# Low parts of y and of the output weights on VectorE instead of GpSimd, their casts behind the newest gate's tanh, and the seventh pair's y split where it is gated

## The chip, the core and the metric

The kernel runs on one core of one Trainium2 chip. The metric is the device time of one execution in microseconds (us), as the median of several runs. Engines are named as the profile names them: PE is TensorE (matmuls; PEld are its weight loads), DVE is VectorE, ACT is ScalarE, POOL is GpSimd, SP is SyncE, whose queue issues the transfers.

## The reference, cut to what matters

A sequence of 1024 positions with 1024 channels passes through two residual layers and a final RMS norm, all in float32.

```python
# layer 0, RG-LRU (width 1536 = 12 blocks of 128)
u = h @ w_in;  xb, gate = u[..., :1536], u[..., 1536:]
xc = causal_depthwise_conv(xb, conv_w, conv_b)          # 4 taps
r = sigmoid(block_diag_linear(xc, wa, ba));  i = sigmoid(block_diag_linear(xc, wx, bx))
log_a = -8 * r * softplus(-a_param);  a = exp(log_a)
hs = associative_scan(a, sqrt(-expm1(2 * log_a)) * i * xc)
x = x + (hs * silu(gate)) @ w_out
# layer 1, forgetting attention (16 heads of 64)
q, k, v, gate, f = split(h @ w_in)
cum = cumsum(log_sigmoid(f + b_f))
p = softmax(mask(q k' / 8 + cum_q - cum_k));  o = p v
x = x + (o * silu(gate)) @ w_out
return rms_norm(x, final_g)
```

## The kernel before, in words

**Split matmuls.** Every float32 operand of a large matmul is held as two parts: a high part (`to_hi`, a cast to `fp32r`, mostly on ACT) and a low part (`to_lo`, the source less the high part, one subtraction of two SBUF tensors). A product is then three matmuls, high by high (L111), low weight by high (L112) and high weight by low (L113). So each weight tile needs a transfer, a cast and a subtraction before PE can use it, and PE waits for the subtraction one matmul later than for the cast. Weight tiles rotate through four buffers each of `wh` and `wl`, and three of `wf`, where the transfers land.

**Order.** The kernel is written as Python loops, and a scheduler puts each engine's instructions into one fixed list by its own timeline. On the chip each engine works through its list strictly in order. `tc.issue_after(i)` is a bound for the scheduler: what stands under it is placed behind instruction `i`.

**Layer 0** runs a loop over the 12 blocks, `n` from 0 to 11. Iteration `n` computes `ups` (block n's half of `u`, 48 matmuls), the two gates of block n-1 (`gates`: four `gate` products of three matmuls, each read by a tanh on ACT, first `th` in two halves, then `ti` in two halves; the products rotate through two PSUM banks, so that the first `ti` product needs the first `th` tanh done), block n-2's output y = a * sg (`outputs`: high part `yh` on ACT, low part `yl`), the convolution of block n (`us` on DVE, `xc`, three taps, `xch`, `xcl`), and `gps`, the gate half of `u` for block n-1. From n = 3 on, each iteration also does two pieces of the output projection of an earlier pair of blocks (`project_out`, one piece per `take(fill, 4)`): a piece loads one tile of output weights (`out_weights`: two transfers, the cast `wh` on ACT, the low part `wl`) and does four `ops` products of six matmuls. The first piece stands between `ups` and `gps`, the second behind `gps`. The recurrence (`recur`: activations L315 to L320, products L318, L319, L321 and the scan L322 on DVE) and `silu` (L299 to L301) run beside it.

**Layer 1** goes head by head, with `hd` from 0 to 15. The scores are made twice, once as `S` for the row maxima (L664 on DVE, an exponential on ACT at L667) and once transposed as `ST`, whose exponential `p` (L734, L737) gets masked on POOL (L742), split into `ph` and `pl` on DVE and multiplied by v into `O`. `gated` multiplies the output `yo` of a pair of heads by its gate on POOL (L777). For pairs 0 to 6 the result goes to DRAM (`y1d`), and `load_y` brings it back later and splits it into `yhh` and `yhl` for the last projection; only pair 7's is split where it stands, with `split_y`. `late`, a generator that runs beside head 14, loads the output weights of pairs 6 and 7, casts them (`woh` on ACT) and makes their low parts (`wol` on POOL), and then calls `load_y` for pair 6.

Of the kernel before, what the change touches and what calls it, by code (L numbers as in the profile page):

```python
# [33 lines left out]
def f32(ap):  # L34
    return ap.bitcast(F32)
# [3 lines left out]
def trunk(ctx: ExitStack, tc: tile.TileContext, xt, w0, wg, wo0, pc, gn, w1, wv, wf, bf, wo1, out):  # L39
    nc = tc.nc  # L40
# [31 lines left out]
    def to_hi(hi, src, eng, scale=None):  # L72
        if eng is nc.scalar:
            if scale is None:
                nc.scalar.copy(hi, src)  # L75
            else:
                nc.scalar.activation(hi, src, AF.Copy, scale=scale)
        elif eng is nc.gpsimd:
            nc.gpsimd.tensor_scalar(hi, src, 1.0 if scale is None else scale, 0.0, ALU.mult, ALU.add)
        elif scale is None:  # L80
            eng.tensor_copy(hi, src)  # L81
        else:
            eng.tensor_scalar(hi, src, scale, None, ALU.mult)

    def to_lo(lo, src, hi, eng):
        return eng.tensor_tensor(lo, src, f32(hi), ALU.subtract)  # L86
# [30 lines left out]
    def drain(gen):  # L117
        for _ in gen:
            pass
# [5 lines left out]
    def gemm(*args):  # L125
        drain(gemm_steps(*args))
# [42 lines left out]
    with ExitStack() as l0:  # L169
# [8 lines left out]
        def long(tag, dtype=F32, bufs=1):  # L178
            return tmp.tile([P, SEQ], dtype, tag=tag, name=tag, bufs=bufs)
# [101 lines left out]
        def gates(n):  # L281

            s = state[n]
            s["t"] = long("th"), long("ti")
            for j, b_ in enumerate((hba, hbx)):
                w = tuple(z[:, j] for z in s["w"])
                for cs in halves:
                    pt = ps.tile([P, HALF], F32, tag="O", name="gate")
                    gemm(pt, [(w, tuple(z[:, cs] for z in s["x"]))])
                    s["last"] = nc.scalar.activation(  # L290
                        s["t"][j][:, cs], pt, AF.Tanh, bias=b_[:, n : n + 1], scale=0.5
                    )

# [31 lines left out]
        def outputs(n, parts=(slice(0, SEQ),), gate=itertools.repeat(None)):  # L325
            s = state.pop(n)
            y = tuple(ypool.tile([P, SEQ], F32R, tag=z, name=z) for z in ("yh", "yl"))
            for cs, _ in zip(parts, gate):
                a_ = s["a"][:, cs]
                nc.vector.tensor_tensor(a_, a_, s["sg"][:, cs], ALU.mult)  # L330
                yh, yl = (z[:, cs] for z in y)
                to_hi(yh, a_, nc.scalar)
                to_lo(yl, a_, yh, nc.vector if len(parts) > 1 else nc.gpsimd)
            ys.append(y)

        def out_weights(g, d0):

            wt = wpool.tile([P, 4, P], F32, tag="wf", name="wf", bufs=3)
            for j in range(2):
                nc.sync.dma_start(wt[:, 2 * j : 2 * j + 2], wo0[d0 + j, :, 2 * g : 2 * g + 2])  # L340
            hi = wpool.tile([P, 4, P], F32R, tag="wh", name="wh")
            lo = wpool.tile([P, 4, P], F32R, tag="wl", name="wl")
            to_hi(hi, wt, nc.scalar)
            to_lo(lo, wt, hi, nc.vector if held is None else nc.gpsimd)
            return [[(hi[:, 2 * j + i], lo[:, 2 * j + i]) for i in range(2)] for j in range(2)]

        def project_out(g):

            for d0 in range(0, KT, 2):
                for db, w in enumerate(out_weights(g, d0), d0):  # L350
                    for h, cs in enumerate(halves):
                        pt = ps.tile([P, HALF], F32, tag="g", name="ops")
                        gemm(pt, zip(w, [tuple(z[:, cs] for z in p) for p in ys[2 * g : 2 * g + 2]]))
                        x = xs[h][db]
                        nc.vector.tensor_tensor(x, x, pt, ALU.add)  # L355
                        yield
# [3 lines left out]

        ys, fill, held = [], iter(()), {}
        for n in range(NB):
            wu = first[0] if n == 0 else list(weights(w0[n]))
            if n == 1:
# [24 lines left out]
            if n % 2 and n > 1:  # L391
                fill = itertools.chain(fill, project_out((n - 3) // 2))
# [15 lines left out]
        for h in range(2):  # L408
            product(gps[:, h], h, wn)
        outputs(NB - 2)  # L410
        held = None
        drain(fill)
        recur(NB - 1, halves)
        outputs(NB - 1, halves, silu(state[NB - 1], gps, halves))
# [17 lines left out]
        wl = [w for d0 in range(0, KT, 2) for w in out_weights(NB // 2 - 1, d0)]  # L432
        for h, cs in enumerate(halves):
            y = [tuple(z[:, cs] for z in p) for p in ys[-2:]]
            hT[h] = [pair() for k in range(KT)]
            parts = split_x(h, 1)
# [29 lines left out]
    with ExitStack() as l1:  # L466
# [126 lines left out]
        parts = [at.tile([HEADS, SEQ], F32R, tag=t, name="cp") for t in ("ph", "pl")]  # L593
# [177 lines left out]
        def gated(hd, c, sub=slice(0, HALF)):  # L771

            if hd % 2 == 0:
                return
            pair = hd // 2
            yo = yos[pair, c][:, sub]
            nc.gpsimd.tensor_tensor(  # L777
                yo, yo, sgs[pair][:, c * HALF + sub.start : c * HALF + sub.stop], ALU.mult
            )
            if hd == 15:  # L780
                split_y(c, yo, nc.vector, sub)
            else:
                nc.sync.dma_start(y1d[c, pair], yo)

        def chain(*gens):
            for g in gens:
                yield from g

        last, seen, lag = [None], [None], []
# [20 lines left out]
        def load_y(c, pairs):  # L810
            for pair in pairs:
                y = at.tile([P, HALF], F32, tag="xp", name="y", bufs=3)
                nc.sync.dma_start(y, y1d[c, pair])
                split_y(c, y, nc.vector)
# [77 lines left out]
        def late():  # L892

            for half in range(2):
                wh, wl = (kqpool.tile([P, 8, P], F32R, tag=f"qk{p}{half}", name=f"wo{p}") for p in "hl")
                for b in range(2):
                    wt = wpool.tile([P, 4, P], F32, tag="wf", name="wf", bufs=3)
                    for d in range(2):
                        nc.sync.dma_start(wt[:, 2 * d : 2 * d + 2], wo1[half * 4 + b * 2 + d, :, 6:8])
                    sl = slice(4 * b, 4 * b + 4)  # L900

                    with tc.issue_after(seen[0].ins):
                        to_hi(wh[:, sl], wt, nc.scalar)
                    to_lo(wl[:, sl], wt, wh[:, sl], nc.gpsimd)
                    yield
                late_w.extend([(wh[:, 2 * d + k], wl[:, 2 * d + k]) for k in range(2)] for d in range(4))
            for c in range(2):
                load_y(c, [6])
                yield

        drain(kq_units(0, (1,)))
        fill = g_units(0)
        for _ in range(4):
# [5 lines left out]
        for hd in range(HEADS):  # L919
            pair = hd // 2  # L920
            if hd % 2 == 0:
                if hd < 14:
                    fill = kq_units(pair + 1)
            elif pair < 6:
                fill = g_units(pair + 1)
            if hd == 12:
                fill = chain(fill, g_units(7))
            if hd == 13:
                load_y(0, range(3, 6))
                load_y(1, range(6))  # L930
                fill = partial()
# [27 lines left out]
        fill = chain(final(0, 0), final(0, 1))  # L959
# [79 lines left out]
```

## Time and profile before

| | |
|---|---|
| median of 3 runs | 1170.67 us (1169.18 to 1171.21) |
| the profiled execution's own time | 1169.07 us |
| its span | 1167.4 us |
| mean granted PE clock | 0.992 |
| busy: PE, DVE, ACT, POOL | 1135.0, 821.0, 596.3, 394.5 us |

The profiled execution is one run, and its 1169.07 us lie 1.6 us below the median. Layer 0 fills the first 460 us or so of the span, layer 1 the rest. The profile counts 1278 instructions on DVE and 361 on POOL; the busy time of an engine includes time in which an instruction has begun but is held up by something outside its engine.

### The profile page before, as it was taken

Reading aid. Unit: us, or ns where it says so; the run is one execution under the profiler, and the core shown is the slowest. Engines: PE = TensorE matmul, PEld = TensorE weight load, DVE = VectorE, ACT = ScalarE, POOL = GpSimd, SP = SyncE. Lnnn points to the kernel's source line nnn. Section 1 sums busy time; section 2 is a strip of 40 time slices with the busy share of each in tenths; the row PEclk is TensorE's granted clock in tenths of the full one; section 3 lists DMA queues with packets and bytes.
Section 4 is the critical chain, followed back from the end, with each engine's and each line's share of the span. In section 5 each row is a group of like instructions: output and inputs, shape, how many; then the busy total and the mean of one; then the engine's idle time right before and its main releaser. Section 6 shows DMA issues by size and latency. Waiting matters only on the chain.

```text
span 1167.4 us, 15836 instructions
## 1 busy us (share of the span) xinstructions
PE 1135.0 (97%) x5653; PEld 949.2 (81%) x5653; DVE 821.0 (70%) x1278; ACT 596.3 (51%) x1010; POOL 394.5 (34%) x361
## 2 busy tenths in 40 slices
PE   9998999999999999999999999999999999999996
PEld 7786888888888887978888988889888898787795
DVE  7588746766567779566877767777577775676677
ACT  8386445364453667454554545545455454444343
POOL 1233332342323302342333332333333233143445
PEclk9999999999999999999999999999999999999998
DMA  6111120111111124441343423433234331656544
GB/s 209 51 41 40 51 59 28 59 50 41 55 36 55 54 68 153 108 132 46 92 118 81 102 64 92 119 85 89 64 91 110 90 84 60 184 161 171 160 134 145
DMA packets 63278, 105.95 MB, mean 91 GB/s; under 512 B 8856, under 2 KB 27928, under 8 KB 63200
## 3 DMA queue, kind: packets, MB, share of 16 engines
q1 hardware_dynamic: 63200, 104.95, 32.1%
q8 instruction: 44, 0.72, 0.3%
q14 instruction: 34, 0.28, 0.1%
HBM read 63.30 MB, written 16.45 MB: 68 GB/s over the span
## 4 chain that ended last, share of the span: by engine, by line
PE 48%; DVE 6%; ACT 2%; issue 2%; DMA 1%; DVEq 0%; POOL 0%; ACTq 0%; SPq 0%
PE gps L111 6%; PE gps L112 6%; PE gps L113 6%; PE O L763 3%; PE S L660 3%; PE S L659 3%; PE ST L728 3%; PE O L762 3%; PE ST L729 2%; PE vps L524 2%; PE vps L522 2%; PE vps L523 2%; PE ops L112 2%; PE ops L113 2%; PE ops L111 2%
## 5 line engine op out<-in xcount | busy, mean ns | idle before, releaser
L86 POOL TENSOR_TENSOR wl<-wf,wh 128x512 fp32r<-128x512 f32 (+2 forms) x148 | 216.5, 1467 | 418.3 <-ACT wh L75 376.2
L111 PE MATMUL gps<-hh,wh 128*128 128x512 f32 x576 | 226.9, 394 | 0.6 <-DVE qkl L560 0.5
L112 PE MATMUL gps<-hh,wl 128*128 128x512 f32 x576 | 227.4, 395 | 0.0
L113 PE MATMUL gps<-hl,wh 128*128 128x512 f32 x576 | 227.2, 394 | 0.0
L75 ACT CAST wh<-wf 128x512 fp32r<-128x512 f32 (+2 forms) x156 | 94.1, 607 | 134.6 <-PE ops L113 38.8
L667 ACT ACTIVATE S<-S,st 128x128 f32<-128x128 f32 (+7 forms) x128 | 91.4, 714 | 111.5 <-DVE st L664 110.6
L113 PEld LDWEIGHTS gps<-hl,wh 128*128 128x128 f32 x576 | 108.4, 188 | 24.6 <-issue 0.5
L81 DVE CAST ph<-p 128x512 fp32r<-128x512 f32 (+2 forms) x130 | 83.9, 655 | 61.4 <-ACT p L734 32.3
L111 PEld LDWEIGHTS gps<-hh,wh 128*128 128x128 f32 x576 | 108.5, 188 | 22.6 <-DVE qkl L560 0.9
L112 PEld LDWEIGHTS gps<-hh,wl 128*128 128x128 f32 x576 | 108.4, 188 | 21.9 <-POOL wl L86 0.3
L86 DVE TENSOR_TENSOR pl<-p,ph 128x512 fp32r<-128x512 f32 (+2 forms) x130 | 115.1, 901 | 2.2
L742 POOL TENSOR_SCALAR_AFFINE_SELECT p<-p 128x128 f32<-128x128 f32 (+1 forms) x128 | 46.9, 384 | 190.4 <-ACT p L734 92.0
L664 DVE CUSTOM_DVE_ANT_0 S<-S,mask 128x128 f32<-128x128 f32 (+7 forms) x128 | 96.6, 758 | 9.9 <-PE S L660 8.9
L355 DVE TENSOR_TENSOR x<-x,ops 128x512 f32<-128x512 f32 x80 | 54.3, 682 | 48.7 <-PE ops L113 48.4
L111 PE MATMUL ups<-hh,wh 128*128 128x512 f32 x192 | 76.3, 397 | 2.6 <-DVE us L265 1.9
L112 PE MATMUL ups<-hh,wl 128*128 128x512 f32 x192 | 75.6, 394 | 0.8 <-POOL wl L86 0.8
L113 PE MATMUL ups<-hl,wh 128*128 128x512 f32 x192 | 76.0, 396 | 0.2
L734 ACT ACTIVATE p<-ST 128x512 f32<-128x512 f32 (+1 forms) x68 | 53.0, 786 | 42.5 <-PE ST L729 39.1
L524 PE MATMUL vps<-wl,hh 128*128 128x256 f32 (+1 forms) x256 | 72.2, 284 | 0.7 <-POOL wl L86 0.7
L522 PE MATMUL vps<-wh,hh 128*128 128x256 f32 (+1 forms) x256 | 72.5, 285 | 0.0
L523 PE MATMUL vps<-wh,hl 128*128 128x256 f32 (+1 forms) x256 | 72.5, 284 | 0.0
L728 PE MATMUL ST<-U,T 128*128 128x512 f32 (+1 forms) x198 | 67.7, 349 | 2.7 <-ACT S L667 2.7
(193 smaller groups left out, 2611.1 us busy)
## 6 DMA issues: line engine op xcount, KB each, us to landing
wf<-in_w SPq DMA_DIRECT2D x100, 256.0 KB
wf<-in_wo SPq DMA_DIRECT2D x64, 128.0 KB
T<-qkh SPq DMA_DIRECT2D x28, 256.0 KB
U<-qkh SPq DMA_DIRECT2D x28, 256.0 KB
x<-in_xt SPq DMA_DIRECT2D x16, 256.0 KB
x1d<-x SPq DMA_DIRECT2D x16, 256.0 KB
wf<-in_wv SPq DMA_DIRECT2D x16, 256.0 KB
xp<-x1d SPq DMA_DIRECT2D x16, 256.0 KB
```

The lines of the kernel that those rows point to most:

```text
L75: nc.scalar.copy(hi, src)
L81: eng.tensor_copy(hi, src)
L86: return eng.tensor_tensor(lo, src, f32(hi), ALU.subtract)
L111: nc.tensor.matmul(o, wh, xh[:, cs], start=i == 0, stop=False)
L112: nc.tensor.matmul(o, wl, xh[:, cs], start=False, stop=False)
L113: nc.tensor.matmul(o, wh, xl[:, cs], start=False, stop=i == len(pairs) - 1)
L522: nc.tensor.matmul(pt, xh, wh, start=k == 0, stop=False)
L523: nc.tensor.matmul(pt, xl, wh, start=False, stop=False)
L524: nc.tensor.matmul(pt, xh, wl, start=False, stop=k == KT - 1)
L664: nc.vector.tensor_tensor_reduce(S[:, :n], S[:, :n], mask[:, SEQ - n :], -1.0, -NEG, ALU.add, ALU.min, accum_out=m)
L667: seen[0] = nc.scalar.activation(S[:, :n], S[:, :n], AF.Exp, bias=f32(m), scale=-1.0, accum_out=sums[:, i : i + 1])
L728: nc.tensor.matmul(A[:, jj, :n], T[s][:, 0, ks], U[s][:, 0, q0:end], start=True, stop=False)
```

## The change

In layer 0, `outputs` now makes `yl` on DVE in every iteration (it was POOL but for the last one), and `out_weights` makes `wl` on DVE in every call (it was POOL but for the last five calls). The casts `wh` of `out_weights` stand under `issue_after` of the newest tanh that `gates` has recorded, which is the second `ti` tanh of the latest gates. In layer 1, `late` makes its four `wol` on DVE; from head 13 on `gated` splits y where it is made, so that pair 6 is no longer written to `y1d` and read back, and `late` has no `load_y` any more.

```diff
@@ gates
-                    s["last"] = nc.scalar.activation(
+                    newest[0] = s["last"] = nc.scalar.activation(
                         s["t"][j][:, cs], pt, AF.Tanh, bias=b_[:, n : n + 1], scale=0.5
                     )
@@ outputs
-                to_lo(yl, a_, yh, nc.vector if len(parts) > 1 else nc.gpsimd)
+                to_lo(yl, a_, yh, nc.vector)
@@ out_weights
-            to_hi(hi, wt, nc.scalar)
-            to_lo(lo, wt, hi, nc.vector if held is None else nc.gpsimd)
+
+            with tc.issue_after(newest[0].ins):
+                to_hi(hi, wt, nc.scalar)
+            to_lo(lo, wt, hi, nc.vector)
@@ layer 0
-        ys, fill, held = [], iter(()), {}
+        ys, fill, held, newest = [], iter(()), {}, [None]
...
-        held = None
@@ gated
-            if hd == 15:
+            if hd >= 13:
                 split_y(c, yo, nc.vector, sub)
             else:
                 nc.sync.dma_start(y1d[c, pair], yo)
@@ late
                     with tc.issue_after(seen[0].ins):
                         to_hi(wh[:, sl], wt, nc.scalar)
-                    to_lo(wl[:, sl], wt, wh[:, sl], nc.gpsimd)
+                    to_lo(wl[:, sl], wt, wh[:, sl], nc.vector)
                     yield
...
-            for c in range(2):
-                load_y(c, [6])
-                yield
-
```

The scheduler rebuilds the lists from this. Three places of them follow. Names carry the numbers of their buffers here, which are the same in both kernels.

**Iteration 6 of layer 0.** Engine ACT, around the `ti` tanh pair of the gates; `wh_1617` is the first piece's output weights, `wh_1655` and `wh_1661` are the weights of `gps`. Before:

```order
L75 CAST wh_1617<-wf_1614 128x512
L290 ACTIVATE th_1546<-gate_1548,hba_108 128x512
L290 ACTIVATE th_1546<-gate_1553,hba_108 128x512
L315 ACTIVATE m2_1719<-th_1546,c2_103 128x1024
L316 ACTIVATE a_1718<-th_1546,nc2_104 128x1024
L317 ACTIVATE th_1546<-a_1718 128x1024
L75 CAST wh_1655<-wf_1653 128x512
L290 ACTIVATE ti_1547<-gate_1558,hbx_109 128x512
L290 ACTIVATE ti_1547<-gate_1563,hbx_109 128x512
L75 CAST yh_1568<-a_1460 128x1024
```

The same place of ACT in the changed kernel:

```order
L317 ACTIVATE th_1546<-a_1718 128x1024
L290 ACTIVATE ti_1547<-gate_1558,hbx_109 128x512
L290 ACTIVATE ti_1547<-gate_1563,hbx_109 128x512
L75 CAST yh_1568<-a_1460 128x1024
L75 CAST wh_1617<-wf_1614 128x512
L75 CAST wh_1655<-wf_1653 128x512
L266 ACTIVATE xc_1598<-us_1597,pct_91 128x1024
L75 CAST wh_1661<-wf_1659 128x512
```

The cast `wh_1617` has moved from ahead of the four tanh to behind them and behind `yh_1568`, and `wh_1655` follows it.

Engine PE, from the last gate matmul on. Before, 13 `ups` matmuls stand between that and the first `ops` matmul; the end of these and what follows:

```order
L112 MATMUL ups_1521<-hh_199,wl_1518 128x512
L113 MATMUL ups_1521<-hl_200,wh_1517 128x512
L111 MATMUL ops_1621<-yh_1052,wh_1617 128x512
L112 MATMUL ops_1621<-yh_1052,wl_1618 128x512
L113 MATMUL ops_1621<-yl_1053,wh_1617 128x512
```

In the changed kernel:

```order
L113 MATMUL gate_1563<-xcl_1347,wgh_1352 128x512
L113 MATMUL ups_1521<-hl_198,wh_1517 128x512
L111 MATMUL ups_1521<-hh_199,wh_1517 128x512
L112 MATMUL ups_1521<-hh_199,wl_1518 128x512
L113 MATMUL ups_1521<-hl_200,wh_1517 128x512
L111 MATMUL ops_1621<-yh_1052,wh_1617 128x512
L111 MATMUL ops_1629<-yh_1052,wh_1617 128x512
L111 MATMUL gps_1665<-hh_169,wh_1655 128x512
L112 MATMUL ops_1621<-yh_1052,wl_1618 128x512
```

Only four `ups` matmuls now lie between the last gate matmul and the first that reads `wh_1617`, and three more until `wl_1618` is read. Iterations 5 and 7 to 11 have the same pattern, iteration 4 has 24 `ups` matmuls there.

Engine DVE, at the same place of the changed kernel (before, `x04` at L355 followed `us_1597`, and `yl_1569` and `wl_1618` were POOL's):

```order
L265 TENSOR_TENSOR us_1597<-ups_1521,rs_168 128x1024
L86 TENSOR_TENSOR yl_1569<-a_1460,yh_1568 128x1024
L86 TENSOR_TENSOR wl_1618<-wf_1614,wh_1617 128x512
L269 SCALAR_TENSOR_TENSOR xc_1598<-us_1597,pct_91,xc_1598 128x1023
```

The low part that PE reads stands behind `us`, which waits for the last `ups` matmul, and behind `yl`.

**Iteration 3 of layer 0**, where the first output weights come. Engine ACT of the kernel before (`wh_843` and `wh_881`, the output weights and the first `gps` weights, stand further ahead there):

```order
L75 CAST wh_957<-wf_954 128x512
L290 ACT_TABLE_LOAD
L290 ACTIVATE th_772<-gate_774,hba_108 128x512
L266 ACTIVATE xc_824<-us_823,pct_91 128x1024
L290 ACTIVATE th_772<-gate_779,hba_108 128x512
L315 ACTIVATE m2_945<-th_772,c2_103 128x1024
L316 ACTIVATE a_944<-th_772,nc2_104 128x1024
L317 ACTIVATE th_772<-a_944 128x1024
L290 ACTIVATE ti_773<-gate_784,hbx_109 128x512
L75 CAST xch_830<-xc_824 128x1024
L320 ACT_TABLE_LOAD
```

And of the changed kernel:

```order
L290 ACT_TABLE_LOAD
L290 ACTIVATE th_772<-gate_774,hba_108 128x512
L290 ACTIVATE th_772<-gate_779,hba_108 128x512
L266 ACTIVATE xc_824<-us_823,pct_91 128x1024
L315 ACTIVATE m2_945<-th_772,c2_103 128x1024
L316 ACTIVATE a_944<-th_772,nc2_104 128x1024
L290 ACTIVATE ti_773<-gate_784,hbx_109 128x512
L290 ACTIVATE ti_773<-gate_789,hbx_109 128x512
L75 CAST wh_843<-wf_840 128x512
L75 CAST wh_881<-wf_879 128x512
```

The two `th` and the two `ti` tanh now stand side by side, and both casts behind them. On PE, the changed kernel has the four gate products (12 matmuls) in a row, and behind them:

```order
L113 MATMUL gate_789<-xcl_651,wgh_656 128x512
L111 MATMUL ops_847<-yh_614,wh_843 128x512
L111 MATMUL ops_855<-yh_614,wh_843 128x512
L111 MATMUL gps_891<-hh_169,wh_881 128x512
L112 MATMUL gps_891<-hh_169,wl_882 128x512
```

Before, 21 `gps` and `ops` matmuls stood between the second and the third gate product, and five between the third and the fourth.

**Head 14 of layer 1.** Engine ACT, before:

```order
L767 COPY yo<-O 64x512
L75 CAST yhh<-y 128x512
L667 ACTIVATE S,sums<-S,st 128x384
L75 CAST woh<-wf 128x512 x3
L734 ACTIVATE p<-ST 128x1024 x2
L75 CAST yhh<-y 128x512
L75 CAST woh<-wf 128x512
```

Engine DVE in the changed kernel at that place (its line numbers past L347 run one or two above those of before):

```order
L691 COPY rc<-tr 8x128
L86 TENSOR_TENSOR wol<-wf,woh 128x512 x3
L81 CAST ph<-p 128x1024
L86 TENSOR_TENSOR pl<-p,ph 128x1024
L81 CAST ph<-p 128x1024
L86 TENSOR_TENSOR wol<-wf,woh 128x512
L665 ISA S,st<-S,mask 128x512
```

On ACT the two `yhh` are gone from here (they stand among head 13's instructions); on DVE the four `wol` are new and the two `yhl<-y` are gone.

## The prediction

> **What bounds the kernel now.** I read the page first, then the busy time by stretches, then what PE waits for.
>
> ```profile
> span 1167.4 us, 15836 instructions
> PE 1135.0 (97%) x5653; PEld 949.2 (81%) x5653; DVE 821.0 (70%) x1278; ACT 596.3 (51%) x1010; POOL 394.5 (34%) x361
> 100.00:120.00 20.00, 17.00 (x66) 12.78 (x65) 16.75 (x14) 16.39 (x20) 7.96 (x3) 0.91 0.11 34
> 200.00:220.00 20.00, 20.00 (x89) 16.28 (x88) 14.98 (x17) 9.84 (x13) 7.51 (x5) 1.00 0.15 47
> 1060.00:1080.00 20.00, 17.61 (x80) 13.39 (x78) 12.50 (x22) 10.57 (x21) 8.76 (x7) 1.00 0.53 158
> 1080.00:1100.00 20.00, 17.65 (x76) 14.17 (x77) 16.29 (x30) 8.04 (x18) 10.12 (x13) 0.91 0.57 171
> ```
>
> PE is the bound, busy 97% of the span. A steady stretch of layer 0 (200 to 220 us, iteration 6) has no gap: 89 matmuls in 20 us, one per 0.225 us, 0.23 us for the 512-column ones. PE's instructions don't change, so the change can only remove waits of PE or make new ones. What can go lies in two places that it touches, around 100 us (iteration 3) and at 1060 to 1090 us (head 14):
>
> ```profile
> 98.95 0.50 PE L111 MATMUL gate<-xch,wgh 128*128 128x512 f32 x1 [1.91 <-ACT th L290]
> 108.34 0.69 PE L111 MATMUL gate<-xch,wgh 128*128 128x512 f32 x1 [2.20 <-ACT ti L290]
> 114.06 0.50 PE L112 MATMUL ups<-hh,wl 128*128 128x512 f32 x1 [0.80 <-POOL wl L86]
> 1071.34 0.50 PE L728 MATMUL ST<-U,T 128*128 128x512 f32 x1 [1.75 <-ACT S L667]
> 1080.09 0.50 PE L762 MATMUL O<-ph,v 128*128 128x512 f32 x1 [0.58 <-DVE ph L81]
> 1082.95 0.27 PE L673 MATMUL mrow<-ident,st 128*4 128x128 f32 x1 [1.66 <-DVE st L664]
> ```
>
> The number in brackets is PE's wait and what ended it. 4.9 us of waits in iteration 3, 4.0 us in head 14. Each place also pays for a slow clock, which the windows show:
>
> ```profile
> 47.05:50.46 3.41, 1.62 (x7) 1.36 (x8) 2.73 (x3) 2.72 (x4) 1.29 (x1) 1.00 0.11 38
> 50.46:53.87 3.41, 3.41 (x17) 2.76 (x16) 2.36 (x3) 1.93 (x2) 0.00 (x0) 1.00 0.26 77
> 105.07:108.49 3.42, 1.22 (x6) 0.69 (x5) 0.56 (x2) 3.38 (x5) 0.00 (x0) 1.00 0.14 38
> 108.49:111.90 3.41, 3.41 (x9) 2.28 (x9) 3.38 (x2) 2.93 (x5) 2.60 (x2) 0.50 0.00 0
> ```
>
> A window of 3.41 us with 1.79 us of idle PE left the next at full clock; one with 2.20 us idle made the next run at 0.50, a loss of up to half of 3.41, 1.7 us. Somewhere between 1.8 and 2.2 us lies the limit. So the old cost is 4.9 + 1.7 = 6.6 us in iteration 3 and 4.0 + 1.7 = 5.7 us in head 14 (its second slow window is the other 0.91 above).
>
> **Part 1: the low parts on DVE, the casts behind the tanh, iterations 5 to 11.** What a low part costs on each engine, and the other prices:
>
> ```profile
> L86 POOL TENSOR_TENSOR yl<-a,yh 128x1024 fp32r<-128x1024 f32 x9 | 21.6, 2404 | 21.1 <-ACT yh L75 21.1
> L86 DVE TENSOR_TENSOR xcl<-xc,xch 128x1024 fp32r<-128x1024 f32 x8 | 9.7, 1217 | 0.0
> L86 DVE TENSOR_TENSOR wl<-wf,wh 128x512 fp32r<-128x512 f32 x5 | 3.3, 680 | 0.0
> 202.38 1.37 ACT L290 ACTIVATE ti<-gate,hbx 128x512 f32<-128x512 f32 x2
> 202.48 1.30 POOL L86 TENSOR_TENSOR wl<-wf,wh 128x512 fp32r<-128x512 f32 x1 [12.31 <-ACT wh L75]
> 202.64 0.39 PE L113 MATMUL gate<-xcl,wgh 128*128 128x512 f32 x1
> 203.56 0.39 PE L113 MATMUL ups<-hl,wh 128*128 128x512 f32 x1
> 203.79 0.40 PE L111 MATMUL ups<-hh,wh 128*128 128x512 f32 x1
> 203.66 1.04 ACT L75 CAST yh<-a 128x1024 fp32r<-128x1024 f32 x1
> 204.59 0.62 ACT L75 CAST wh<-wf 128x512 fp32r<-128x512 f32 x1
> 205.63 0.40 PE L113 MATMUL ups<-hl,wh 128*128 128x512 f32 x1
> 206.06 1.22 DVE L265 TENSOR_TENSOR us<-ups,rs 128x1024 f32<-128x1024 f32 x1 [1.68 <-PE ups L113]
> ```
>
> On its own a 1024-wide low part takes 1.22 us on DVE against 2.40 on POOL, a 512-wide one 0.68 against 1.30. An iteration adds one yl and two wl to DVE, 2.6 us against some 36 (156 matmuls of 0.23); DVE is busy 15 of 20 us, so its load doesn't bind. Its order does.
>
> ACT goes through `ti`, `ti`, `yh`, `wh` one behind the other in the trace as it will after; but after, that `wh` is the weight of the first `ops`. In the trace it ends at 204.59 + 0.62 = 205.21. The last gate matmul starts at 202.64, four `ups` follow up to 203.56, and the next slot of PE is 203.79. Before, there were more `ups` to do, and the `ops` weights had been cast long ago. After, PE waits until 205.25: **1.45 us**. What hid that cast before, the `th` tanh and nine more matmuls, is gone.
>
> Then two `ops` and one `gps` matmul go, to 205.95, and PE needs `wl`. DVE starts `us` 0.43 us behind the last `ups` matmul (206.06 against 205.63), so at 204.0; it ends at 205.2, `yl` at 206.4, `wl` at 207.1: a second wait of 1.15 us. This is its lower bound. The upper one comes from POOL, which starts the low part of the `gps` weights as soon as these are cast, near 205.8:
>
> ```profile
> 109.58 3.30 DVE L321 TENSOR_TENSOR ti<-ti,m 128x1024 f32<-128x1024 f32 x1
> 111.74 5.52 POOL L86 TENSOR_TENSOR wl<-wf,wh 128x512 fp32r<-128x512 f32 x2
> 112.98 3.18 DVE L322 TENSOR_TENSOR_SCAN a<-a,ti 128x1024 f32<-128x1024 f32 x1
> 219.99 2.29 DVE L322 TENSOR_TENSOR_SCAN a<-a,ti 128x1024 f32<-128x1024 f32 x1
> ```
>
> Two-input SBUF work of DVE and POOL takes turns: L321 ends at 112.88, the scan then takes 3.18 us where one without POOL ahead takes 2.29, and the second of the two POOL subtractions ends 1.1 us behind the scan's end. The waiting POOL goes first when DVE's instruction ends. So POOL gets 206.4 to 207.6, DVE's `wl` ends at 208.25, and the second wait is **2.3 us**. I take this value, since the rows show such turns wherever both stand ready; 1.15 stays as the low end.
>
> Seven iterations have this pattern: 7 x (1.45 + 2.3) = **26 us**. The two waits lie within 4.45 us, and nine in ten positions of a 3.41 us window over them hold 2 us or more of idle PE, so a slow window follows most times. It costs at most 1.7 us, less where the second wait reaches into it; I take 1.3: 7 x 0.9 x 1.3 = **8 us** (0 to 12).
>
> "TensorE: Matmul & The Clock Gate" of the Trainium skill, section "HAM oscillation", gives the rule that the clock falls after gaps of over some 3.4 us of idle PE. By it neither wait would slow the clock, and the sum would be 8 us lower. The row at 108.49, slow behind a gap of 2.2 us, speaks against it.
>
> **Part 2: iteration 3.** The new PE list has the four gate products in a row. The rows for ACT:
>
> ```profile
> 92.44 1.28 ACT L290 ACT_TABLE_LOAD   x1
> 97.09 1.24 ACT L266 ACTIVATE xc<-us,pct 128x1024 f32<-128x1024 f32 x1 [2.66 <-DVE us L265]
> 100.08 1.23 ACT L316 ACTIVATE a<-th,nc 128x1024 f32<-128x1024 f32 x1
> ```
>
> Counting from the first gate product's end at 88.9 (87.8, where the products start before too, and four matmuls): table load to 90.2, `th` to 90.9 and 91.5. The third product waits from 89.2 to 90.9, 1.7 us. `us` is behind `yl` on DVE and ends near 91.8; then `xc` to 93.0, two activations to 95.4, two `ti` to 96.7, the cast to 97.3. PE is through with the gates at 92.3 and waits 5.0 us. The `gps` low part on POOL (1.30, beside DVE's taps) costs another 1.3, the `ops` low part behind the taps on DVE 0.8, the slow clock about 1: 9.8 us. Both tanh waits of before go. Net 9.8 - 6.6 = **+3 us** (from -3, if `us` or the casts come early, to +6).
>
> **Part 3: head 14.** What ended the waits there:
>
> ```profile
> 1069.98 0.62 ACT L75 CAST yhh<-y 128x512 fp32r<-128x512 f32 x1 [3.02 <-DMA y<-y1d]
> 1075.02 3.30 DVE L86 TENSOR_TENSOR pl<-p,ph 128x1024 fp32r<-128x1024 f32 x1
> 1077.20 3.98 POOL L86 TENSOR_TENSOR wol<-wf,woh 128x512 fp32r<-128x512 f32 x2
> 1081.13 0.53 POOL L742 TENSOR_SCALAR_AFFINE_SELECT p<-p 128x128 f32<-128x128 f32 x2
> ```
>
> ACT stood 3.0 us before `yhh`, for the read-back of y; the `S` exponential that PE needed was queued behind it. Then `pl` on DVE took 3.30 us for a 1024-wide subtraction, taking turns with POOL's `wol`, and `st` came late. With no read-back and no `wol` on POOL both causes go; two `y1d` writes and two reads leave SP's queue, which nobody misses. What is late next is `wol` itself: three (2.0 us) stand ahead of `ph`, but `woh` comes about 1.8 us earlier than before, so `ph` is no later. In head 13 ACT gains two casts of 0.62 and DVE two subtractions of 0.69, in stretches with idle time on both; 0 to 0.5 us. I take **-5.5** of the 5.7 (to -7, if small waits near go too; -2 if `wol` holds `ph`).
>
> **Sum.** 26 + 8 + 3 - 5.5 = +31.5 us on the profiled 1169.1: 1201 us. The median stood 1.6 us above that execution; I leave this out.
>
> **Rivals.**
> *Faster.* The casts come in time, no new waits appear, and the old ones go: 1169 - 6.6 - 5.7 = 1157. For it speaks that a low part is halved on DVE and takes no turns with POOL's. "GPSIMD Engine Reference", section "Engine selection", has elementwise work on VectorE and not on GpSimd; by that the change gains, and 1157 would be its time. It decides at one point: the `wh` cast must end within four matmuls of the last gate, 1.45 us sooner than ACT's own rows put it. I see no way: 0.06. Partial: waits of 1.45 alone, 10 us, less 12: about 1168, 0.03.
> *Turns without loss.* DVE's `wl` goes ahead of POOL: second wait 1.15, 18 us in all, slow windows half as often, 5 us: 1169 + 18 + 5 + 3 - 5.5 = 1190. Against it stand the scan's rows: 0.2.
> *No slow clock* behind these waits, as by the clock-gate rule: 1193; a pair of waits with matmuls between may count otherwise than one gap: 0.2.
> *More.* The `ops` sums x (L355) stand among more DVE work and free their PSUM bank late; another 1 to 1.5 us per iteration: 1210. The room there is about 2 us: 0.1.
> My forecast: 0.41.
>
> From these: slower by over 0.2% (about what a measurement here can tell from no change) 0.91, within 0.2% 0.03, faster 0.06. The range runs from the case without turns and clock and a full gain in head 14 (1169 + 18 + 2 - 7 = 1182) to the case with more waits (1211).
>
> **What would show it.** Right: the 20 us stretches from 150 to 440 us show PE at about 17 to 18 instead of 20, with waits of `ops` L111 for ACT `wh` near 1.4 us and of L112 for DVE `wl` near 2.3, seven each, granted clock below 1 in most of them; POOL's `yl` gone; near 100 us one wait of some 5 us; no wait over 1 us in head 14. Wrong: PE full in those stretches, which would mean that ACT reaches the cast earlier than its list and these durations allow.

## The result, and the profile after

The changed kernel takes 1209.76 us (median, 1209.18 to 1213.67) where the kernel before took 1169.53 in runs beside it. The ratio is 1.0342, with a 95% interval of 1.0328 to 1.0357. Predicted were 1201 us, with a range of 1182 to 1211: the sign and the mechanism came as forecast, and the loss was 9 us larger than forecast. Lines behind `out_weights` have numbers up to two higher in the changed kernel (L290 is the same, L728 is now L729).

First the page of the changed kernel, then 20 us stretches of iterations 5 to 11 (start and end, length, busy PE, PEld, DVE, ACT, POOL with instruction counts, granted PE clock, DMA share, GB/s):

```profile
span 1207.5 us, 15828 instructions
PE 1152.6 (95%) x5653; PEld 957.2 (79%) x5653; DVE 840.8 (70%) x1311; ACT 596.0 (49%) x1010; POOL 329.2 (27%) x328
```

```profile
200.00:220.00 20.00, 16.90 (x72) 13.04 (x71) 7.89 (x10) 9.81 (x12) 2.60 (x2) 1.00 0.04 14
...
380.00:400.00 20.00, 16.89 (x60) 12.92 (x59) 18.57 (x17) 8.23 (x10) 3.35 (x2) 0.83 0.18 60
```

POOL has lost 33 instructions and 65 us, and PE, which before did 89 matmuls from 200 to 220 us, does 72. An iteration lasts about 41 us, so the loss shows in about every other stretch, as missing PE time and as a clock below 1. Iteration 6 shows how the time goes (start, duration, engine, line, operation; in brackets the idle time before and what ended it):

```profile
215.15 0.40 PE L113 MATMUL ups<-hl,wh 128*128 128x512 f32 x1
215.25 1.03 ACT L75 CAST yh<-a 128x1024 fp32r<-128x1024 f32 x1
...
215.59 1.22 DVE L265 TENSOR_TENSOR us<-ups,rs 128x1024 f32<-128x1024 f32 x1 [0.17 <-PE ups L113]
216.18 1.14 ACT L75 CAST wh<-wf 128x512 fp32r<-128x512 f32 x2
216.73 1.21 DVE L86 TENSOR_TENSOR yl<-a,yh 128x1024 fp32r<-128x1024 f32 x1
216.85 0.73 PE L111 MATMUL ops<-yh,wh 128*128 128x512 f32 x2 [1.31 <-ACT wh L75]
...
217.40 3.35 POOL L86 TENSOR_TENSOR wl<-wf,wh 128x512 fp32r<-128x512 f32 x2 [21.75 <-ACT wh L75]
217.42 0.45 PE L111 MATMUL gps<-hh,wh 128*128 128x512 f32 x1
217.86 1.76 DVE L86 TENSOR_TENSOR wl<-wf,wh 128x512 fp32r<-128x512 f32 x1
...
219.67 0.50 PE L112 MATMUL ops<-yh,wl 128*128 128x512 f32 x1 [1.80 <-DVE wl L86]
```

The last `ups` matmul starts at 215.15. The next matmul needs the cast `wh`, which stands behind `yh` on ACT, and starts 1.70 us later instead of 0.23: a first wait of 1.47 us by the spacing of the starts (the bracket, counted from the end of the matmul, says 1.31). From the `gps` matmul at 217.42 to 219.67 it is 2.25 us instead of 0.23, a second wait of 2.0 us. DVE reaches `wl` at 217.86, behind `us` and `yl`, and then takes 1.76 us for it, since POOL's `wl` of the `gps` weights is at work. The list of PE's waits shows the same pair in all seven iterations (waited for, total us, times, longest); the eighth and longest L111 wait is that of iteration 3:

```profile
PE ops L111 <- ACT wh L75: 13.1, 8, 4.0
PE ops L112 <- DVE wl L86: 12.6, 7, 1.8
```

The slow clock follows as expected. Windows of 3.41 us around iterations 6 and 7:

```profile
216.88:220.29 3.41, 1.61 (x6) 0.99 (x7) 3.41 (x3) 2.10 (x3) 2.89 (x2) 1.00 0.17 56
220.29:223.71 3.42, 3.42 (x10) 2.65 (x9) 3.38 (x4) 0.62 (x1) 0.46 (x1) 0.50 0.72 229
...
257.84:261.25 3.41, 1.21 (x4) 0.67 (x5) 3.41 (x4) 2.53 (x4) 2.46 (x2) 1.00 0.25 74
261.25:264.67 3.42, 3.42 (x9) 2.64 (x9) 3.38 (x3) 0.62 (x1) 0.89 (x1) 0.50 0.65 218
```

A window with 1.80 us of idle PE, and one with 2.20, are each followed by one at half clock. All seven iterations have such a slow window, and one of them (380 to 400 us, clock 0.83 above) has two in a row.

Iteration 3 has the forecast wait of the first `ops` for its cast, behind four gate products in a row; in layer 1 the longest wait near the edited place belongs to head 13 (counted by the `ST` matmuls, 24 in each head up to 14), and head 14 has none over 1 us:

```profile
93.06 0.50 PE L111 MATMUL gate<-xch,wgh 128*128 128x512 f32 x1 [1.66 <-ACT th L290]
98.68 1.22 PE L111 MATMUL ops<-yh,wh 128*128 128x512 f32 x2 [3.95 <-ACT wh L75]
100.78 0.80 PE L112 MATMUL gps<-hh,wl 128*128 128x512 f32 x1 [0.44 <-POOL wl L86]
```

```profile
1058.12 0.50 PE L729 MATMUL ST<-U,T 128*128 128x512 f32 x1 [1.56 <-ACT S L668]
...
1103.98 0.39 PE L729 MATMUL ST<-U,T 128*128 128x256 f32 x1 [0.41 <-ACT S L668]
...
1125.62 0.51 PE L112 MATMUL ops<-yhh,wl 128*128 128x512 f32 x1 [0.66 <-POOL wl L86]
```

The account against the profile before, by the times at which PE starts the same work: the first `fps` matmul of layer 1 starts 42.0 us later (529.5 against 487.5), and PE's work from there to its last matmul takes 2.3 us less. Of the 42.0 us, 24.4 are the two waits in seven iterations, some 12.8 the eight slow windows there (1.6 each, an estimate: half of the time in which PE was busy in them), 1.1 iteration 3, 1.5 a slow window near 50 us that the kernel before just missed; 2.2 is spread.

### The profile page after: what moved, and what is told of

Same layout as the page of the kernel before. It is cut to its first block, busy times and chain, and to the rows that moved or that the text cites. A ratio compares the mean times of both kernels' runs of the same rounds, so it can differ in the third digit from the quotient of the medians.

```text
span 1207.5 us, 15828 instructions
## 1 busy us (share of the span) xinstructions
PE 1152.6 (95%) x5653; PEld 957.2 (79%) x5653; DVE 840.8 (70%) x1311; ACT 596.0 (49%) x1010; POOL 329.2 (27%) x328
## 4 chain that ended last, share of the span: by engine, by line
PE 81%; DVE 9%; ACT 3%; issue 3%; DMA 2%; POOL 1%; SPq 0%; DVEq 0%; ACTq 0%; POOLq 0%
PE gps L112 10%; PE gps L113 10%; PE gps L111 10%; PE ops L112 5%; PE ops L113 4%; PE ops L111 4%; PE ups L113 4%; PE ups L111 4%; PE ups L112 4%; PE O L764 3%; PE ST L729 2%; PE S L661 2%; PE S L660 2%; PE O L763 2%; PE ST L730 2%
## 5 line engine op out<-in xcount | busy, mean ns | idle before, releaser
L86 POOL TENSOR_TENSOR wl<-wf,wh 128x512 fp32r<-128x512 f32 (+2 forms) x130 | 183.2, 1416 | 558.4 <-ACT wh L75 407.8
L111 PE MATMUL gps<-hh,wh 128*128 128x512 f32 x576 | 228.4, 397 | 1.2 <-DVE qkl L561 1.2
L111 PEld LDWEIGHTS gps<-hh,wh 128*128 128x128 f32 x576 | 109.5, 190 | 24.7 <-DVE qkl L561 1.7
L112 PE MATMUL ops<-yh,wl 128*128 128x512 f32 x160 | 68.5, 429 | 12.6 <-DVE wl L86 12.6
L111 PE MATMUL ups<-hh,wh 128*128 128x512 f32 x192 | 76.6, 399 | 3.5 <-DVE us L265 1.9
L111 PE MATMUL ops<-yh,wh 128*128 128x512 f32 x160 | 65.3, 418 | 13.2 <-ACT wh L75 13.1
```

Source lines behind the costliest of these rows:

```text
L111: nc.tensor.matmul(o, wh, xh[:, cs], start=i == 0, stop=False)
L112: nc.tensor.matmul(o, wl, xh[:, cs], start=False, stop=False)
```

## The experiments

Theory: the place of the casts makes the waits; the second wait has DVE's order and a turn behind POOL in it. Rivals: that low parts on DVE cost by themselves, and that the scheduler's new order does.

**Free casts.** The tie alone is taken out of the changed kernel.

```diff
-            with tc.issue_after(newest[0].ins):
-                to_hi(hi, wt, nc.scalar)
+            to_hi(hi, wt, nc.scalar)
```

> The kernel after, with only the tie of the output weights' casts to the newest gate's tanh taken away; yl and both wl stay on DVE, layer 1 stays as after. Theory (the place of the casts): in the list of ACT these casts move back ahead of ti and yh, and the first ops of an iteration find their weights ready. Both waits of iterations 5 to 11 (1.47 and 2.01 us each, 24.4 us in all) and the slow windows behind them (some 12.8 us) go, layer 0 costs what it did before give or take 3 us (the order near iteration 3 is another one again), and layer 1 keeps its gain of about 4 us: 1166 us (1162 to 1171). Rival (the load of DVE): it is the low parts on DVE that come late, and they are still there; the waits of ops for wl on DVE remain and the time stays over 1185 us. Rival (a half each): only the first wait goes, 7 x 1.47 us and a part of the slow clock: about 1192 us.

Measured: 1160.48 us beside 1171.25, ratio 0.9903 (0.9886 to 0.9921). The page and the stretches of iteration 3 and iteration 6:

```profile
span 1158.8 us, 15813 instructions
PE 1131.8 (98%) x5653; PEld 949.3 (82%) x5653; DVE 830.1 (72%) x1311; ACT 596.4 (51%) x1010; POOL 334.2 (29%) x328
```

```profile
100.00:120.00 20.00, 19.97 (x88) 15.97 (x87) 16.50 (x19) 15.53 (x19) 5.16 (x2) 1.00 0.19 57
200.00:220.00 20.00, 20.00 (x88) 16.22 (x87) 18.43 (x19) 9.27 (x10) 4.54 (x2) 1.00 0.20 63
```

PE is full in iteration 6 with the same 1311 instructions on DVE. So the load of DVE isn't the cause, and the tie costs some 50 us. The time is also below the expected range: near iteration 3, where the kernel before lost time, PE is full as well. This was not expected and is followed up below.

**Layer 1's part alone**, in the kernel before.

```diff
-            if hd == 15:
+            if hd >= 13:
...
-                    to_lo(wl[:, sl], wt, wh[:, sl], nc.gpsimd)
+                    to_lo(wl[:, sl], wt, wh[:, sl], nc.vector)
...
-            for c in range(2):
-                load_y(c, [6])
-                yield
```

> The kernel before, with layer 1's part of the change alone: y of the seventh pair split where it is gated, no read-back of it, wol on DVE. Theory: the three waits of head 14 (1.75, 0.58 and 1.66 us) and its slow window shrink to some waits of under 1 us, as in the trace of after, where this stretch lost some 4.4 us instead of 8.0: 1169.5 - 4 = 1165.5 us (1163 to 1167.5). The prediction's own term was -5.5, which would give 1164. Rival: what the stretch gained in the trace of after comes from elsewhere (layer 0 ends later there, and loads for layer 1 have longer to land); then the waits of head 14 stay, and the time is 1169 us.

Measured: 1167.92 us beside 1171.25, ratio 0.9969 (0.9958 to 0.9981): 3.3 to 3.6 us less, a little under the expected 4 (the time lies 0.4 us above the expected range) and below the predicted 5.5. The rival, no gain, is out.

**The low parts back on POOL, the tie kept.**

```diff
-                to_lo(yl, a_, yh, nc.vector)
+                to_lo(yl, a_, yh, nc.vector if len(parts) > 1 else nc.gpsimd)
...
-            to_lo(lo, wt, hi, nc.vector)
+            to_lo(lo, wt, hi, nc.vector if held is None else nc.gpsimd)
...
+        held = None
```

> The kernel after, with layer 0's yl and output wl back on POOL as before; the casts stay behind the newest gate's tanh, layer 1 as after. Theory (the place of the casts): the first wait stays at 1.4 us, since it ends with the cast of wh on ACT. The second now ends with POOL: yl starts with the end of yh's cast and takes 2.4 us there, wl 1.3 us behind it, and is through some 0.4 us later than on DVE (220.0 against 219.6 in iteration 6 of the trace of after), so a second wait of 2.2 to 2.4 us instead of 1.8; the slow windows stay. 1212 us (1206 to 1219), so DVE in place of POOL is a small gain where the casts are late. Rival (the load of DVE): with DVE relieved of the low parts the waits go or halve, and the time is 1165 to 1190 us.

Measured: 1227.38 us beside 1171.25, ratio 1.0468 (1.0445 to 1.0490). The sign is the theory's, the size 15 us over it and outside its range. Iteration 6:

```profile
225.15 2.37 POOL L86 TENSOR_TENSOR yl<-a,yh 128x1024 fp32r<-128x1024 f32 x1 [21.01 <-ACT yh L75]
225.64 0.73 PE L111 MATMUL ops<-yh,wh 128*128 128x512 f32 x2 [1.31 <-ACT wh L75]
...
227.28 5.73 DVE L269 SCALAR_TENSOR_TENSOR xc<-us,pct,xc 128x1023 f32<-128x1023 f32 x3 [1.69 <-ACT xc L266]
227.47 6.70 POOL L86 TENSOR_TENSOR wl<-wf,wh 128x512 fp32r<-128x512 f32 x3
...
229.77 0.79 PE L112 MATMUL ops<-yh,wl 128*128 128x512 f32 x1 [3.11 <-POOL wl L86]
```

The first wait is again 1.31 us. POOL begins `wl` at 227.47, and PE gets it at 229.77, 2.3 us later where 1.30 is its length alone: a DVE tap (one of the three multiply-adds of the convolution, L269) had begun at 227.28 and went first. The expectation had left out this turn. Iteration 3 lost more too, where the longest wait for a cast is now 6.9 us and not 4.0:

```profile
PE ops L111 <- ACT wh L75: 16.1, 8, 6.9
```

Against the changed kernel that makes 1.3 us in seven iterations, 9 us, and 3 in iteration 3. The medians differ by 18 us, the ratios to the kernel before by some 15; the rest goes with more slow windows (18 in this trace, 11 in that of the changed kernel, those in the last 20 us left out). So with tied casts, DVE in place of POOL is worth 15 to 18 us, not 3.

**The tie to `th` instead of the last tanh.**

```diff
-                    newest[0] = s["last"] = nc.scalar.activation(
+                    s["last"] = nc.scalar.activation(
...
+                    if j == 0:
+                        newest[0] = s["last"]
```

> The kernel after, with the output weights' casts tied to the newest gate's th tanh (the first two halves of a gate) instead of to the last of its tanhs; nothing else. Theory (the place of the casts): ACT's list now has two of these casts ahead of ti and one behind yh, so the first ops of iterations 5 to 11 find wh and wl ready; both waits and the slow windows of layer 0's steady part go (some 37 us), while iteration 3 with its four gate products in a row and a wait of 4 to 5 us is the same as after: 1173 us (1169 to 1178), some 3 to 7 us above the kernel with free casts. Rival: any tie of the casts to the gate costs, since wl on DVE then stands behind us and yl all the same: the second wait of some 2 us stays in seven iterations, 1190 us or more.

Measured: 1167.36 us beside 1171.25, ratio 0.9966 (0.9950 to 0.9982). The two waits are gone with the casts still tied: what matters is that ACT does `wh` before `ti` and `yh`. The time lies 1.6 us below the expected range: iteration 3 came out better, since its cast too is no longer behind `ti`; the wait of 3.95 us there has become this one:

```profile
PE ops L111 <- ACT yh L75: 1.3, 1, 1.3
```

It is still 6.9 us slower than the kernel with free casts; no run takes that apart.

**Nothing for POOL beside DVE.** In the changed kernel the `gps` weights' low parts go to DVE too.

```diff
-                wn = list(weights(w0[NB + n - 1]))
+                wn = list(weights(w0[NB + n - 1], lo_eng=nc.vector))
```

> The kernel after, with the low parts of the gps weights on DVE too, so that POOL has nothing to do in layer 0's steady part while DVE works; the casts stay tied. Theory (turns): in iteration 6 of the trace of after, DVE's wl for the ops took 1.76 us and not 0.68, because POOL's low part of the gps weights went first. Without it wl ends 1.0 us sooner: second wait 0.8 us instead of 1.8 in seven iterations, first wait as before 1.4 us, and somewhat less slow clock (12.8 us become 8 to 12): 1210 - 7 - 2 = 1201 us (1195 to 1206). Rival (DVE's wl is slow or late by itself, behind us and yl): the second wait stays at 1.8 us, and with two more subtractions for DVE in each iteration the time is 1209 to 1216 us.

Measured: 1202.39 us beside 1171.69, ratio 1.0265 (1.0249 to 1.0281). Iteration 6, then the group of all `wl` on DVE, here and in the changed kernel (minimum/median/maximum in ns, start of the first and last):

```profile
218.82 0.73 PE L111 MATMUL ops<-yh,wh 128*128 128x512 f32 x2 [1.30 <-ACT wh L75]
220.57 0.50 PE L112 MATMUL ops<-yh,wl 128*128 128x512 f32 x1 [0.73 <-DVE wl L86]
```

```profile
L86 DVE TENSOR_TENSOR wl<-wf,wh x46: 665/683/693, 4.4 to 475.0; 128x512 fp32r<-128x512 f32 x46
```

```profile
L86 DVE TENSOR_TENSOR wl<-wf,wh x26: 665/687/1781, 4.0 to 483.7; 128x512 fp32r<-128x512 f32 x26
```

The theory's 1201 us held. With POOL out of the way there no `wl` on DVE takes over 0.69 us, and the second wait falls from 1.80 to 0.73 while the first stays. The turn behind POOL was 1.07 us of the second wait, DVE's order the rest.

**Which low part cured iteration 3.** Both kernels have free casts and layer 1 as changed; in the one only `wl` is on DVE, in the other only `yl`. Against the kernel with free casts:

```diff
-                to_lo(yl, a_, yh, nc.vector)
+                to_lo(yl, a_, yh, nc.vector if len(parts) > 1 else nc.gpsimd)
```

> The kernel with free casts (1160.5 us), but with yl back on POOL; wl of the output weights on DVE, layer 1 as after. The kernel with free casts came out 5 us faster than expected, since the waits of 4.9 us near iteration 3 and the slow window behind them were gone too. Theory (wl on DVE moves the gate products): PE's list near iteration 3 reads here as with free casts (the gate's products there in pieces of 2, 4 and 6, the third beginning 18 or 19 gps matmuls behind the last ops), so the waits stay away: 1161 us (1158 to 1164). Rival: yl on DVE is what made us and xc come in time there; then 5 to 7 us of waits are back: 1167 us.

```diff
-            to_lo(lo, wt, hi, nc.vector)
+            to_lo(lo, wt, hi, nc.vector if held is None else nc.gpsimd)
...
+        held = None
```

> The kernel with free casts (1160.5 us), but with the output weights' wl back on POOL; yl on DVE, layer 1 as after. Theory (wl on DVE moves the gate products): PE's list near iteration 3 reads here nearly as before the change, with the same gate products in the same places, so the waits of th and ti (1.9 and 2.2 us) and the slow window are back, and only layer 1's 3.5 us are gained: 1167.5 us (1165 to 1170). Rival (yl on DVE is the cure): no wait over 1 us near iteration 3, 1161 us.

Measured: `wl` alone 1168.65 us, ratio 0.9975 (0.9963 to 0.9987); `yl` alone 1162.00 us, ratio 0.9916 (0.9900 to 0.9931), both beside 1171.69. The theory of the moved gate products is wrong, the rival right: `yl` does it, with the order of PE's matmuls there nearly as before the change. DVE, POOL and a `ti` tanh of ACT near iteration 3, before:

```profile
86.44 2.62 DVE L86 TENSOR_TENSOR wgl<-wgf,wgh 128x256 fp32r<-128x256 f32 x1
88.99 2.30 DVE L319 SCALAR_TENSOR_TENSOR ti<-ti,xc 128x1024 f32<-128x1024 f32 x1
...
92.65 3.28 DVE L322 TENSOR_TENSOR_SCAN a<-a,ti 128x1024 f32<-128x1024 f32 x1
95.86 1.19 DVE L265 TENSOR_TENSOR us<-ups,rs 128x1024 f32<-128x1024 f32 x1
...
85.66 3.12 POOL L86 TENSOR_TENSOR yl<-a,yh 128x1024 fp32r<-128x1024 f32 x1 [5.23 <-ACT yh L75]
...
107.60 0.69 ACT L290 ACTIVATE ti<-gate,hbx 128x512 f32<-128x512 f32 x1
```

and with `yl` on DVE:

```profile
88.05 0.42 DVE L86 TENSOR_TENSOR wgl<-wgf,wgh 128x256 fp32r<-128x256 f32 x1
88.39 1.22 DVE L319 SCALAR_TENSOR_TENSOR ti<-ti,xc 128x1024 f32<-128x1024 f32 x1
89.52 1.22 DVE L86 TENSOR_TENSOR yl<-a,yh 128x1024 fp32r<-128x1024 f32 x1
...
91.79 1.21 DVE L265 TENSOR_TENSOR us<-ups,rs 128x1024 f32<-128x1024 f32 x1
92.93 2.28 DVE L322 TENSOR_TENSOR_SCAN a<-a,ti 128x1024 f32<-128x1024 f32 x1
...
102.26 0.68 ACT L290 ACTIVATE ti<-gate,hbx 128x512 f32<-128x512 f32 x1
```

POOL's `yl` held `wgl` for 2.2 us and L319 for 1.1. On DVE the same subtraction costs 1.22 us and holds nothing. `us` starts 4.1 us earlier, and the held time is only a part of that: the scheduler's new list also puts `us` ahead of the scan (L322), which took 3.28 us in front of it before. On ACT, `xc` is then early, and the new list has the second `ti` tanh (102.26 us, 107.60 before) ahead of the two table loads that it stood behind. So it is shown that `yl` on DVE removes these waits; how much of that is the held time and how much the new order of DVE's and ACT's lists isn't, since no run changes the one without the other. With `yl` on POOL (`wl` alone) the scan stands ahead of `us` again, L319 takes 3.43 us, and the waits for `th` and `ti` are back (1.8 and 2.3 us). What `yl` on DVE gains here, some 6 us beside 3.5 in layer 1, is the larger part of the gain that the tie hid.

**Layer 1 in halves**, in the kernel before: `wol` on DVE alone, and the split alone.

```diff
-                    to_lo(wl[:, sl], wt, wh[:, sl], nc.gpsimd)
+                    to_lo(wl[:, sl], wt, wh[:, sl], nc.vector)
```

> The kernel before, with wol on DVE as the only change; the seventh pair's y is written and read back as before. Theory (two causes in head 14): the S exponential behind yhh still waits for the read-back, so the wait of ST of 1.75 us stays; pl no longer takes turns with POOL's wol, so the waits for ph and st (0.58 and 1.66 us) and the slow window behind them go: 3.5 us less, 1167.5 us (1166 to 1169.5) beside 1171 for before, and about what both edits give together (1167.9). Rival (one cause): the late read-back is what shifted the rest; the waits for ph and st stay, and the time is 1171 us.

```diff
-            if hd == 15:
+            if hd >= 13:
...
-            for c in range(2):
-                load_y(c, [6])
-                yield
```

> The kernel before, with the other half of layer 1's part alone: the seventh pair's y is split where it is gated and not read back; wol stays on POOL. Both halves together gave 1167.9 us and wol alone 1168.4, so what is left for the split is 0.5 us if the two add up. Theory (two causes): the wait of ST of 1.75 us near 1071 us goes, since ACT no longer stands before yhh; the waits for ph and st and the slow window behind them stay, since pl still takes turns with wol on POOL: 1169.8 us (1168.5 to 1171). Rival (the two add up): 1171 us, no different from before. Rival (the read-back shifted the rest): all the waits of head 14 go, 1167 us or less.

Measured: `wol` alone 1168.38 us, ratio 0.9974 (0.9963 to 0.9985); the split alone 1171.63 us, ratio 0.9998 (0.9987 to 1.0010), both beside 1171.69. The first lies in its theory's range; the second lies above the theory's range and at the rival's 1171, no gain. The waits of PE in head 14, with `wol` alone and then with the split alone, and DVE there:

```profile
1072.60 0.50 PE L728 MATMUL ST<-U,T 128*128 128x512 f32 x1 [1.94 <-ACT S L667]
1077.85 0.50 PE L762 MATMUL O<-ph,v 128*128 128x512 f32 x1 [0.30 <-DVE ph L81]
```

```profile
1084.95 0.79 PE L763 MATMUL O<-pl,v 128*128 128x512 f32 x1 [3.59 <-DVE pl L86]
```

```profile
1079.14 5.75 DVE L86 TENSOR_TENSOR pl<-p,ph 128x1024 fp32r<-128x1024 f32 x1
```

With `wol` alone the wait for the read-back stays (1.94 us) and those behind `pl` go. With the split alone that wait goes, and `pl` is held longer than before: 5.75 us, with a wait of 3.59 for it. So what POOL does beside `pl` is the cost that counts; what the split adds to `wol` on DVE, 0.5 us, cannot be told from nothing. POOL's partner in the hold needn't be `wol` itself. In the kernel before, `pl` starts at 1075.02 and takes 3.30 us, and this POOL instruction, the scaling of `sg`, is at work then, right behind the first two `wol`:

```profile
1074.38 2.85 POOL L704 TENSOR_TENSOR sg<-sg,recb 64x1024 f32<-64x1024 f32 x1
```

With `wol` alone on DVE the same `sg` runs from 1073.66 to 1076.04, `pl` starts at 1077.83, and it takes 1.23 us.

## Why the prediction was right, and where its sizes were off

**Part 1, the waits.** Forecast 1.45 and 2.3 us in seven iterations, 26 us; measured 1.47 and 2.0, 24.4 us. The first came out of ACT's list and its durations. The second was 0.3 too large: POOL began at 217.40, while DVE still worked on `yl`, so `wl` was held 1.07 us and not 1.2, and `us` began 0.44 us behind the start of the last `ups` matmul as supposed. That the free casts and the casts behind `th` remove both waits shows the cause. "SBUF — State Buffer" of the Trainium skill, section "Who interferes with whom", says that a DVE instruction with two SBUF inputs and one of POOL that reads SBUF hold off each other for a whole instruction; the 687 ns median and 1781 ns maximum of `wl`, against 693 with POOL idle, agree. The rival of turns without loss (1190) falls with it.

**Part 1, the slow clock.** This is the term that was mis-sized: 8 us forecast, some 12.8 measured. The 1.3 us per iteration supposed that the second wait reaches into the slow window. It hardly does: the window that trips holds the second wait alone (1.8 us idle, three iterations) or with the end of the first (2.2 to 2.4, four), and the slow one behind it is full of matmuls in four of the seven iterations (220.29 to 223.71 is one) and holds 0.3 to 0.8 us of idle PE in the other three, so it loses nearly all of 1.7 us. And not nine in ten but all seven iterations have one, one of them two. The rival without slow clock (1193) is out: "TensorE: Matmul & The Clock Gate" of the Trainium skill, section "HAM oscillation", puts the limit at gaps of over some 3.4 us, and here gaps of 1.5 and 2.0 us were followed by half clock in each of seven iterations, so the measurement decides.

**Part 2, iteration 3.** Forecast +3 net, measured +1.1: the same `ups` matmuls start 2.06 us later than before ahead of it and 3.14 behind it. The wait for `wh` was 3.95 us where 5.0 was forecast: the gate products came some 2 us later than supposed, so `us` was already done and `xc` followed `th` on ACT at once. The wait for POOL's low part was 0.44 and not 1.3, and none came for the low part behind the taps. Against that the slow clock was put too low: two windows in a row are slow, 97.41 to 104.24 us with 1.72 us of idle PE in them, up to 2.6 us where about 1 was forecast.

**Part 3, head 14.** Forecast -5.5. Over heads 13 and 14 the idle and slow time of PE falls from 8.0 to 4.4 us in the trace, 3.6 less, and alone layer 1's part is worth 3.3 to 3.6 us in the medians. Head 14 itself came nearly as forecast: by the starts of the same matmuls it takes 4.7 us less, and no wait there is over 1 us. The term that was put too low is head 13: forecast 0 to 0.5 us for its new casts and subtractions, in this trace 1.6 more than before. There the wait for the `S` exponential is 1.56 us (0.90 in the kernel before), and one of 0.66 for `ph` is new. The first comes ahead of the new casts, which begin at 1086.7, and is 0.88 with layer 1's part alone; its cause stays open. "Both causes go" put 1.75 us on the read-back; the split alone gained nothing. And the row of `wol` that the prediction shows, from 1077.20, cannot have begun the hold of `pl`, which had started 2.2 us earlier, beside `sg`.

**The rivals.** 1210 us was the price of the case "more", but its mechanism is not what happened: the trace has no wait of PE for the `ops` sums in layer 0's loop. What the forecast lacked is the clock (4.8 us more), layer 1 (2.3 us gained by the starts and not 5.5), the slow window near 50 us (1.5) and the spread 2.2, less some 3.5 by which the waits and iteration 3 were put too high; together some 8 of the 9 us. The upper end of the range was set by this case, so that the time fell inside it, by 1 us, is in part luck. The rival "faster", 1157 us, is near what the change gives without the tie: 1160.5 measured. Its condition, a `wh` cast in time, was named rightly as the point that decides. "GPSIMD Engine Reference" of the Trainium skill, section "Engine selection", which sends such subtractions to VectorE, agrees with three pairs of runs here: 1160.5 and 1162.0 against 1167.9 with free casts, 1209.8 against 1227.4 with tied ones; `wl` by itself (1168.7) gained nothing.

The best kernel of the study is that with free casts, 1160.48 us, 0.97% under the kernel before (interval 0.79 to 1.14%).

## What to carry to other kernels

Before a cast is tied behind another instruction, count what stands between that instruction and the first user of the cast on each engine: here four matmuls, 0.9 us, on PE, against the casts `yh` and `wh` behind the last tanh on ACT, which end 1.5 us too late. Read the cost of an engine that shares its work with another from the instructions beside it, too: `yl` on POOL cost DVE more (3.3 us in `wgl` and L319) than doing it itself (1.22). And when one edit of a change adds a large loss, try the change without it: the others were worth 1% here.

## What was not expected of the hardware

The same wait falls on either side of the clock's limit. In every kernel PE waits for `us` near 47 us. Before, the window there had 1.62 us of busy PE (1.79 idle) and the next one ran at full clock; in the changed kernel a window with 1.61 was followed by half clock, and this one as well:

```profile
46.21:49.63 3.42, 1.49 (x5) 0.61 (x4) 1.57 (x2) 1.52 (x3) 0.40 (x1) 1.00 0.23 79
49.63:53.04 3.41, 3.41 (x9) 2.67 (x8) 2.19 (x3) 3.23 (x3) 0.90 (x1) 0.50 0.26 82
```

In the eleven traces this wait of 1.9 us (3.2 in one) was followed by half clock in six and not in five. So where the windows stand against the program decides whether a given wait pays up to 1.7 us on top. But idle time alone is no sharp limit, and what trips reaches below the prediction's 1.8 to 2.2 us. With the windows laid out by the recorded steps of the clock and the last 20 us of each trace left out, every window with 1.85 us of idle PE or more was followed by half clock. Below that both happen: 1.82 was followed by full clock (`wol` alone, from 45.96 us), but 1.71 and 1.58 by half clock (no POOL beside DVE, from 217.83 and 337.30 us). The ends of matmuls are modelled in the profile, which can move these figures somewhat.

Once the clock is at half, less is needed to keep it there. In all traces, each slow window with 0.78 us of idle PE or more was followed by another slow one, and each with 0.60 or less by full clock. That is how one iteration, and iteration 3, came to two in a row.

The executions of one kernel differ by some 5 us (layer 1's part alone: 1165.6 to 1170.3); whether the windows' place is the reason is not shown.

One subtraction `pl` of 1.22 us was held until it had taken 5.75, while POOL ended the `sg` instruction and went through four more. Why DVE did not get its turn after the first of them stays open.
